# A transformer trunk on one core: other places for split weights, smaller first loads, and the last tokens in four pieces

## The chip, the cores and the metric

The kernel runs on one core of a Trainium2 chip. The metric is the device time of one execution in microseconds (us): the median of several runs, lower is better. Beside the timed runs one execution was taken by the hardware profiler; all rows below are from that one.

## What is computed

One sequence of 256 tokens with 1,024 features passes two layers: causal attention (16 heads) with a SwiGLU, then an mLSTM (8 heads) with a second SwiGLU. Every sub-layer has an RMS norm before it and a residual add behind it; a last RMS norm ends the trunk. All arrays are float32. Cut to what matters here:

```python
def swiglu(xn, w_gate_up, w_down):
    gu = jnp.einsum('bsd,df->bsf', xn, w_gate_up)
    g, u = gu[..., :D_FF], gu[..., D_FF:]          # D_FF = 2816
    return jnp.einsum('bsf,fd->bsd', jax.nn.silu(g) * u, w_down)

h = h + moba_mixer(rmsnorm(h, attn_norm[0]), attn_w_qkv[0], attn_w_o[0], cos, sin)
h = h + swiglu(rmsnorm(h, ffn_norm[0]), ffn_w_gate_up[0], ffn_w_down[0])
h = h + mlstm_mixer(rmsnorm(h, mlstm_norm[0]), mlstm_w_in[0], mlstm_b_gates[0], mlstm_head_norm[0], mlstm_w_out[0])
h = h + swiglu(rmsnorm(h, ffn_norm[1]), ffn_w_gate_up[1], ffn_w_down[1])
return rmsnorm(h, final_norm)
```

## The kernel before

**Weights.** All weights are cut into units of 128 x 1024 floats (512 KB), listed by `unit_names` in the order of their use. A unit is loaded by SyncE's queue (SP) into one of 4 `raw` buffers (`load`, L133 to L144). Then ScalarE (ACT) rounds it to `wh` (L159) and VectorE (DVE) makes the rest, `wl` = raw - `wh` (L150): a float32 value as a sum of two numbers of the type float32r, which TensorE (PE) multiplies fast. `wh` and `wl` rotate through 8 buffers each of 4,096 bytes per partition (L155). Activations are split in the same way: `xh` and `xl` (L206, L207) hold the normed input, `hh` and `hl` (L652, L653) a hidden block of a SwiGLU. A product is three matmuls (`mm3`, L188): high x high, high x low, low x high.

**Where the tiles lie.** Pools are laid one behind another, with small filling tiles (`pad`) between some of them. In the built program each `raw`, `wh` and `wl` buffer begins at a multiple of 256 bytes in its partition; `xh`, `xl`, `hh` and `hl` begin 192 bytes past such a multiple.

**The order of TensorE's work** is the order in which the code is written; for most of the program a scheduler orders the other engines' instructions. A matmul has a stationary operand (loaded before it, 128 x 128) and a moving one (128 x 256 or 128 x 512).

- At the start 16 small matmuls warm TensorE; `first_block` then multiplies x, piece by piece (k = 0 to 7, 128 features each), with attention's first query and key weights: per k four blocks of six matmuls of 256 columns, each needing its quarter of the weight unit. x is not normed here. The norm's square sums (`square`, L211) are taken on ScalarE and added up on GpSimd (POOL, L219, L221), and the factor is applied to the results.
- A SwiGLU (`ffn`) has 22 hidden blocks. A **pair block** (`pair_block`) makes one block's gate and up values: 48 matmuls of 256 columns with `xh`/`xl` moving and weights stationary. A **down step** multiplies one hidden block with its part of the down matrix. In the first SwiGLU it is 24 matmuls of 256 columns with `hh`/`hl` moving and weights stationary. In the second the result stands with tokens in partitions, so that the last norm can work along the free dimension: 12 matmuls of 512 columns with weights moving and `hh`/`hl` stationary (`tok_tiles`, L390). Pair blocks and down steps follow each other in turns; the down step of block j - 6 runs beside block j. The last down steps stand alone behind the last pair block.
- The end (`finish_last`, L395): for each half of the tokens (t = 0, 1) and each half of the columns (c = 0, 1; one PSUM bank each) the last two down steps are done, then ScalarE squares and sums the bank. The two sums are added on VectorE (L408), GpSimd takes the power -1/2 (L410), ScalarE and VectorE scale one half each (L414, L416), and SP stores both (L418).

```python
            for c in range(2):
                cs = slice(c * 512, (c + 1) * 512)
                for i, (u, h) in enumerate(steps):
                    tok_tiles(acc, u, h, t, c, i == len(steps) - 1)
                sq = fp.tile([P, 512], F32, name="fsq", tag="fsq")
                nc.scalar.activation(sq, acc[2 * t + c], AF.Square, scale=1.0 / 32.0, accum_out=ss[:, c:c + 1])
```

Of the kernel before, what the change touches and what calls it, by code (L numbers as in the profile page):

```python
# [9 lines left out]
F32 = mybir.dt.float32  # L10
F32R = mybir.dt.float32r
BF16 = mybir.dt.bfloat16
AF = mybir.ActivationFunctionType
ALU = mybir.AluOpType
PSUM = bass.MemoryType.PSUM

P = 128
S = 256
NF = 8
NJ = 22  # L20
EPS = 1e-6
# [7 lines left out]
LAG = 6  # L29
# [10 lines left out]

V_ATTN, V_FFN0, V_MLSTM, V_FFN1, V_HEAD, V_BIAS, V_END = 0, 8, 16, 24, 32, 40, 56

def unit_names():
# [31 lines left out]
def trunk_kernel(ctx: ExitStack, tc: tile.TileContext, x, w, wg, fw, tab, out):  # L77
    nc = tc.nc
    names = unit_names()
# [14 lines left out]
    w_pool = ctx.enter_context(tc.tile_pool(name="wsplit", bufs=WBUFS))  # L94
    xp = ctx.enter_context(tc.tile_pool(name="xp", bufs=1))
    sm = ctx.enter_context(tc.tile_pool(name="small", bufs=2))
# [23 lines left out]
    XV = xp.tile([P, V_END + NF * S], F32, name="XV")  # L120
# [6 lines left out]
    split = {}  # L127

    def pieces(c):
        return (slice(0, S), slice(S, 1024)) if c == 0 else (slice(0, 1024),)  # L130

    def load(upto):
        while len(raws) < min(upto, len(names)):  # L133
            c = len(raws)
            raw = raw_pool.tile([P, 1024], F32, name="raw", tag="raw")
            if c < NF:
                o = V_END + c * S
                o = slice(o if c else 0, o + S)
                nc.sync.dma_start(out=XV[:, o], in_=x[:, o])
            for sl in pieces(c):  # L140
                nc.sync.dma_start(out=raw[:, sl], in_=w[c][:, sl])
            if c == 5:
                nc.sync.dma_start(out=tab_t, in_=tab)
            raws.append(raw)  # L144
# [7 lines left out]
    def prefetch(upto, lag=0):  # L152
        for c in range(len(split), min(upto, len(names))):
            load(c + RAW - 1)
            wh, wl = (w_pool.tile([P, 1024], F32R, name=a, tag=a) for a in ("wh", "wl"))  # L155
            split[c] = (wh, wl)
            cuts = (0, S, 512, 1024) if c == 0 else (0, 512, 1024) if c == 1 else (0, 1024)
            for sl in map(slice, cuts, cuts[1:]):
                nc.scalar.copy(wh[:, sl], raws[c][:, sl])  # L159
                lows.append((c, sl))  # L160
                if len(lows) > lag:
                    low(*lows.pop(0))
                if c < NF and sl.start == 0:
                    n0.feed(c)
        while len(lows) > lag:
            low(*lows.pop(0))
# [15 lines left out]
    mhalf = const.tile([P, 2], F32, name="mhalf")  # L182
# [5 lines left out]
    def mm3(o, a, b, start, stop):  # L188

        mm(o, a[0], b[0], start, False)  # L190
        mm(o, a[0], b[1], False, False)
        mm(o, a[1], b[0], False, stop)

    class Norm:
# [15 lines left out]
        def square(self, f):  # L210

            xs = X[:, f:f + 2].rearrange("p f t -> p (f t)")
            if self.ssum is None:
                self.ssum = sm.tile([P, 512], F32, name="ssum", tag="ssum", bufs=1)
                nc.scalar.activation(self.ssum, xs, AF.Square)
            else:
                sq = sm.tile([P, 512], F32, name="sq", tag="sq")
                nc.scalar.activation(sq, xs, AF.Square)
                nc.gpsimd.tensor_add(self.ssum, self.ssum, sq)  # L219
            if f == NF - 2:  # L220
                nc.gpsimd.tensor_add(self.ssum[:, 0:S], self.ssum[:, 0:S], self.ssum[:, S:512])  # L221

        def mean(self):
            ms = acc_tile()
# [162 lines left out]
        n.feed(7)  # L387
        return n

    def tok_tiles(acc, u, h, t, c, last):  # L390

        sl, cs = slice(t * P, (t + 1) * P), slice(c * 512, (c + 1) * 512)
        mm3(acc[2 * t + c], (h[0][:, sl], h[1][:, sl]), (u[0][:, cs], u[1][:, cs]), False, last)

    def finish_last(acc, steps, fwb, fp):  # L395

        for t in range(2):
            ss = sm.tile([P, 4], F32, name="ss", tag="fss")
            y = fp.tile([P, 1024], F32, name="yout", tag="yout")
            for c in range(2):  # L400
                cs = slice(c * 512, (c + 1) * 512)
                for i, (u, h) in enumerate(steps):
                    tok_tiles(acc, u, h, t, c, i == len(steps) - 1)
                sq = fp.tile([P, 512], F32, name="fsq", tag="fsq")
                nc.scalar.activation(sq, acc[2 * t + c], AF.Square, scale=1.0 / 32.0, accum_out=ss[:, c:c + 1])
                if c == 0:
                    nc.vector.tensor_mul(y[:, cs], acc[2 * t], fwb[:, cs])
            nc.vector.scalar_tensor_tensor(out=ss[:, 2:3], in0=ss[:, 0:1], scalar=EPS, in1=ss[:, 1:2],  # L408
                                           op0=ALU.add, op1=ALU.add)
            nc.gpsimd.tensor_tensor(out=ss[:, 3:4], in0=ss[:, 2:3], in1=mhalf[:, 0:1], op=ALU.pow)  # L410
            for c in range(2):
                cs = slice(c * 512, (c + 1) * 512)
                if c == 0:
                    nc.scalar.activation(y[:, cs], y[:, cs], AF.Copy, scale=ss[:, 3:4])  # L414
                else:
                    nc.vector.scalar_tensor_tensor(out=y[:, cs], in0=acc[2 * t + 1], scalar=ss[:, 3:4],  # L416
                                                   in1=fwb[:, cs], op0=ALU.mult, op1=ALU.mult)
                nc.sync.dma_start(out=out[t * P:(t + 1) * P, cs], in_=y[:, cs])  # L418


    n = n0 = Norm(V_ATTN)
# [45 lines left out]
    with ExitStack() as actx:  # L467
# [147 lines left out]
        acc = []  # L615
        blocks = [tok_block("av", 2 * i, n, v_evict, lambda *a: main.later(A_D6, *a)) for i in range(2)]
        parts = {0: [blocks[0]], 1: [islice(blocks[1], V1), blocks[1]]}
# [14 lines left out]
        n = finish(acc, [(unit("ao", 3, 1), ot.pop(7))], V_FFN0)  # L632


    def ffn(l, n, fp, col):
        hid = {}
        last_phase = col is None
        if last_phase:
            fwb = fp.tile([P, 1024], F32, name="fwb", bufs=1)
# [19 lines left out]
        acc = []  # L659

        def down(j):
            u = unit(f"d{l}", j // 2, j % 2)
            if not acc:
                acc.extend(acc_tile() for _ in range(4))
                if last_phase:

                    for b in range(4):
                        t, c = b // 2, b % 2
                        for i in range(4):
                            nc.tensor.matmul(acc[b][:, i * P:(i + 1) * P], lhsT=X[:, 4 * c + i, t * P:(t + 1) * P],  # L670
                                             rhs=ident, start=i == 0, stop=False, is_transpose=True,
                                             skip_group_check=True)
            if last_phase:
                for b in range(4):
                    tok_tiles(acc, u, hid[j], b // 2, b % 2, False)
                hid.pop(j)
            else:
                out_tiles(acc, u, hid.pop(j), j == 0, False)

        nd = 0  # L680
        for j in range(4, NJ):
# [3 lines left out]
            b = ps_tile() if j > 4 else acc_tile()  # L685
# [3 lines left out]
        last = (NJ - 2, NJ - 1) if last_phase else (NJ - 1,)  # L689
# [12 lines left out]
    with ExitStack() as mctx:  # L702
# [188 lines left out]
        acc = []  # L891
# [127 lines left out]
```

## Time and profile before

| | |
|---|---|
| median of 3 runs | 607.2 us (607.06 to 607.92) |
| the profiled execution | 605.8 us, of which 604.0 us lie between its first and last instruction (the span) |
| TensorE matmul | 590.7 us busy (98% of the span), 4,524 matmuls |
| VectorE, ScalarE, GpSimd | 415.8, 340.9 and 77.9 us busy |
| granted TensorE clock | 0.996 in the mean |
| DMA engines | 58.7% of their time in transfers |

"Busy" counts an instruction from its start to its end. Matmuls overlap: one that is shown with 0.28 us is followed by the next after 0.11 or 0.12 us, so a busy share near 100% doesn't say that TensorE is at its peak. What a matmul costs in a row of matmuls is the interval from its start to the start of the next.

### The profile page before, as it was taken

Reading aid. Unit: us, or ns where it says so; the run is one execution under the profiler, and the core shown is the slowest. Engines: PE = TensorE matmul, PEld = TensorE weight load, DVE = VectorE, ACT = ScalarE, POOL = GpSimd, SP = SyncE. Lnnn points to the kernel's source line nnn. Section 1 sums busy time; section 2 is a strip of 40 time slices with the busy share of each in tenths; the row PEclk is TensorE's granted clock in tenths of the full one; section 3 lists DMA queues with packets and bytes.
Section 4 is the critical chain, followed back from the end, with each engine's and each line's share of the span. In section 5 each row is a group of like instructions: output and inputs, shape, how many; then the busy total and the mean of one; then the engine's idle time right before and its main releaser. Section 6 shows DMA issues by size and latency. Waiting matters only on the chain.

```text
span 604.0 us, 11573 instructions
## 1 busy us (share of the span) xinstructions
PE 590.7 (98%) x4524; PEld 561.2 (93%) x4524; DVE 415.8 (69%) x663; ACT 340.9 (56%) x611; POOL 77.9 (13%) x81
## 2 busy tenths in 40 slices
PE   8997999999999999999999999999999999999995
PEld 7987998999999999999999878999999999999984
DVE  5899898797866666566388678858776656556532
ACT  7645999767544444445275478846754444444412
POOL 2574320042000000000031300114100000000000
PEclk9999999999999999999999999999999999999999
DMA  8778965358655656555428868343955555565401
GB/s 312 286 216 260 263 200 159 140 180 305 214 196 189 207 179 206 183 201 190 163 81 302 255 218 222 110 141 117 308 175 200 178 187 197 175 194 190 141 0 69
DMA packets 36342, 116.39 MB, mean 193 GB/s; under 512 B 4544, under 2 KB 7360, under 8 KB 36288
## 3 DMA queue, kind: packets, MB, share of 16 engines
q1 hardware_dynamic: 36288, 115.66, 58.7%
q8 instruction: 35, 0.57, 0.4%
q14 instruction: 19, 0.16, 0.1%
HBM read 105.15 MB, written 1.05 MB: 176 GB/s over the span
## 4 chain that ended last, share of the span: by engine, by line
PE 83%; DVE 5%; ACT 4%; DMA 3%; issue 2%; SPq 1%; POOL 1%; POOLq 0%; ACTq 0%; DVEq 0%
PE ps L186 46%; PE acc L186 36%; DMA raw<-w 2%; DVE wl L150 2%; DMA stk<-u 1%; ACT wh L159 1%; ACT p L535 1%; ACT p L545 1%; DVE xl L207 1%; DVE u L449 1%; DVE VT L507 0%; PE ps L555 0%; SPq L452 0%; POOL sh L487 0%; POOL qk L488 0%
## 5 line engine op out<-in xcount | busy, mean ns | idle before, releaser
L150 DVE TENSOR_TENSOR wl<-raw,wh 128x1024 fp32r<-128x1024 f32 (+2 forms) x199 | 244.1, 1233 | 109.5 <-ACT wh L159 106.9
L159 ACT CAST wh<-raw 128x1024 fp32r<-128x1024 f32 (+2 forms) x199 | 205.5, 1038 | 184.9 <-PE ps L186 102.7
L186 PE MATMUL ps<-xh,wh 128*128 128x256 f32 x864 | 242.4, 281 | 0.8 <-ACT wh L159 0.8
L186 PE MATMUL ps<-xh,wl 128*128 128x256 f32 x864 | 241.0, 279 | 0.5 <-DVE wl L150 0.5
L186 PE MATMUL ps<-xl,wh 128*128 128x256 f32 x864 | 240.7, 279 | 0.0
L186 PEld LDWEIGHTS ps<-xh,wh 128*128 128x128 f32 x864 | 163.0, 189 | 2.1 <-ACT wh L159 1.2
L186 PEld LDWEIGHTS ps<-xh,wl 128*128 128x128 f32 x864 | 163.7, 189 | 1.1 <-DVE wl L150 1.1
L186 PEld LDWEIGHTS ps<-xl,wh 128*128 128x128 f32 x864 | 163.0, 189 | 0.7
L186 PE MATMUL acc<-hh,wh 128*128 128x256 f32 x176 | 48.6, 276 | 0.0
L186 PE MATMUL acc<-hl,wh 128*128 128x256 f32 x176 | 48.6, 276 | 0.0
L186 PE MATMUL acc<-hh,wl 128*128 128x256 f32 x176 | 48.6, 276 | 0.0
L219 POOL TENSOR_TENSOR ssum<-ssum,sq 128x512 f32<-128x512 f32 x12 | 20.5, 1708 | 198.6 <-issue 163.7
L644 DVE TENSOR_TENSOR tgu<-ps,R 128x512 f32<-128x512 f32 x42 | 28.6, 690 | 20.9 <-PE ps L186 20.9
L186 PE MATMUL acc<-wh,xh 128*128 128x512 f32 x96 | 39.0, 406 | 0.0
L186 PE MATMUL acc<-wh,xl 128*128 128x512 f32 x96 | 37.8, 393 | 0.0
L186 PE MATMUL acc<-wl,xh 128*128 128x512 f32 x96 | 37.7, 392 | 0.0
L186 PE MATMUL acc<-wh,hh 128*128 128x512 f32 x88 | 34.7, 394 | 0.0
L186 PE MATMUL acc<-wl,hh 128*128 128x512 f32 x88 | 34.7, 394 | 0.0
L186 PE MATMUL acc<-wh,hl 128*128 128x512 f32 x88 | 34.3, 390 | 0.0
L186 PEld LDWEIGHTS acc<-hl,wh 128*128 128x128 f32 x176 | 33.0, 188 | 0.0
L186 PEld LDWEIGHTS acc<-hh,wl 128*128 128x128 f32 x176 | 33.0, 188 | 0.0
L186 PEld LDWEIGHTS acc<-hh,wh 128*128 128x128 f32 x176 | 33.0, 188 | 0.0
(180 smaller groups left out, 853.8 us busy)
## 6 DMA issues: line engine op xcount, KB each, us to landing
raw<-w SPq DMA_DIRECT2D x195, 512.0 KB, 4.2
stk<-u SPq DMA_DIRECT2D x24, 192.0 KB, 4.3
stk<-u SPq DMA_DIRECT2D x24, 128.0 KB, 4.2
stk<-u SPq DMA_DIRECT2D x24, 64.0 KB, 3.6
out<-yout SPq DMA_DIRECT2D x4, 256.0 KB, 2.2
XV<-x SPq DMA_DIRECT2D x7, 128.0 KB, 6.2
tab_t<-tab SPq DMA_DIRECT2D x1, 708.0 KB, 6.9
fwb<-fw SPq DMA_DIRECT2D x1, 512.0 KB, 3.5
```

The source lines that it names most:

```text
L150: nc.vector.tensor_sub(wl[:, sl], raws[c][:, sl], wh[:, sl].bitcast(F32))
L159: nc.scalar.copy(wh[:, sl], raws[c][:, sl])
L186: nc.tensor.matmul(o, lhsT=lhsT, rhs=rhs, start=start, stop=stop, skip_group_check=True)
L207: nc.vector.scalar_tensor_tensor(out=self.l[:, f], in0=X[:, f], scalar=wc, in1=self.h[:, f].bitcast(F32), op0=ALU.mult, op1=ALU.subtract)
L219: nc.gpsimd.tensor_add(self.ssum, self.ssum, sq)
L449: nc.vector.tensor_sub(u[:, 512:1024], mv, u[:, 0:512].bitcast(F32))
L535: nc.scalar.activation(pt[:, sl], pt[:, sl], AF.Exp, bias=mx[:, t:t + 1], scale=-1.0, accum_out=ss[:, t:t + 1])
L545: nc.scalar.activation(pt[:, sl], pt[:, sl], AF.Copy, scale=ss[:, t:t + 1])
L644: nc.vector.tensor_mul(t.rearrange("p (g t) -> p g t", g=2), bank.rearrange("p (g t) -> p g t", g=2), n.R2())
```

## The change

Four parts. (1) The split buffers become 4,352 bytes long; in the units listed in `MOVING` (down units 0 to 15 of the second SwiGLU) the data begin 128 bytes into the buffer. (2) Weight units 0 and 1 are loaded in three pieces (256, 256 and 512 columns) and split in three; x's first two pieces are issued from ScalarE's queue. (3) The first norm's square sums are added on VectorE. (4) In `finish_last` the second half of the tokens is done in four pieces of 256 columns, in turns in the two banks. Each piece's sum is added to the running one, each piece is multiplied by the norm's weights before the factor is known, and the factor is applied at the end: for t = 0 by VectorE with one store, for t = 1 by VectorE (672 columns, stored by SP) and ScalarE (352 columns, stored from its own queue).

```diff
+MOVING = tuple(("d1", j // 2, j % 2) for j in range(NJ - LAG))
...
     def pieces(c):
-        return (slice(0, S), slice(S, 1024)) if c == 0 else (slice(0, 1024),)
+        return (slice(0, S), slice(S, 512), slice(512, 1024)) if c < 2 else (slice(0, 1024),)
...
-                nc.sync.dma_start(out=XV[:, o], in_=x[:, o])
+                (nc.scalar if c < 2 else nc.sync).dma_start(out=XV[:, o], in_=x[:, o])
...
-            wh, wl = (w_pool.tile([P, 1024], F32R, name=a, tag=a) for a in ("wh", "wl"))
+            o = 32 if names[c] in MOVING else 0
+            wh, wl = (w_pool.tile([P, 1088], F32R, name=a, tag=a)[:, o:o + 1024] for a in ("wh", "wl"))
             split[c] = (wh, wl)
-            cuts = (0, S, 512, 1024) if c == 0 else (0, 512, 1024) if c == 1 else (0, 1024)
+            cuts = (0, S, 512, 1024) if c < 2 else (0, 1024)
...
+            eng = nc.vector if self.col == V_ATTN else nc.gpsimd
...
-                nc.gpsimd.tensor_add(self.ssum, self.ssum, sq)
+                eng.tensor_add(self.ssum, self.ssum, sq)
             if f == NF - 2:
-                nc.gpsimd.tensor_add(self.ssum[:, 0:S], self.ssum[:, 0:S], self.ssum[:, S:512])
+                eng.tensor_add(self.ssum[:, 0:S], self.ssum[:, 0:S], self.ssum[:, S:512])
...
+    def tok_tiles(acc, u, h, t, cs, last):
+
+        sl, c = slice(t * P, (t + 1) * P), cs.start // 512
+        o = acc[2 * t + c][:, cs.start - c * 512:cs.stop - c * 512]
+        mm3(o, (h[0][:, sl], h[1][:, sl]), (u[0][:, cs], u[1][:, cs]), False, last)
...
+            parts = ((0, 512), (512, 1024)) if t == 0 else ((0, S), (512, 768), (S, 512), (768, 1024))
+            for i, cs in enumerate(slice(*p) for p in parts):
+                for j, (u, h) in enumerate(steps):
+                    tok_tiles(acc, u, h, t, cs, j == len(steps) - 1)
+                a = acc[2 * t + cs.start // 512][:, cs.start % 512:(cs.stop - 1) % 512 + 1]
                 sq = fp.tile([P, 512], F32, name="fsq", tag="fsq")
-                nc.scalar.activation(sq, acc[2 * t + c], AF.Square, scale=1.0 / 32.0, accum_out=ss[:, c:c + 1])
-                if c == 0:
-                    nc.vector.tensor_mul(y[:, cs], acc[2 * t], fwb[:, cs])
...
+                nc.scalar.activation(sq[:, 0:cs.stop - cs.start], a, AF.Square, scale=1.0 / 32.0,
+                                     accum_out=ss[:, i:i + 1])
+
+                if i > 0:
+                    nc.vector.scalar_tensor_tensor(out=ss[:, 3 + i:4 + i], in0=ss[:, i:i + 1],
+                                                   scalar=EPS if i == 1 else 0.0,
+                                                   in1=ss[:, 0:1] if i == 1 else ss[:, 2 + i:3 + i],
+                                                   op0=ALU.add, op1=ALU.add)
+                nc.vector.tensor_mul(y[:, cs], a, fwb[:, cs])
+            n = 2 + len(parts)
+            nc.gpsimd.tensor_tensor(out=ss[:, 7:8], in0=ss[:, n:n + 1], in1=mhalf[:, 0:1], op=ALU.pow)
+            rows = out[t * P:(t + 1) * P]
+            cut = 672 if t else 1024
+            nc.vector.tensor_scalar(y[:, 0:cut], y[:, 0:cut], ss[:, 7:8], None, op0=ALU.mult)
+            nc.sync.dma_start(out=rows[:, 0:cut], in_=y[:, 0:cut])
+            if t:
+                nc.scalar.activation(y[:, cut:], y[:, cut:], AF.Copy, scale=ss[:, 7:8])
+                nc.scalar.dma_start(out=rows[:, cut:], in_=y[:, cut:])
```

By the built program's addresses, the data of units 0 to 15 now begin at 128 past a multiple of 256 bytes; every other tile that a matmul reads keeps its place modulo 256. The 16 split buffers begin at multiples of 256 that are in turns even and odd.

How the change moves instructions on three engines follows from the built programs; line numbers are each program's own.

ScalarE at the program's start, before:

```order
L116 ACT_TABLE_LOAD
L116 ACTIVATE dummy<-warm 128x1
L206 ACTIVATE xh<-XV 128x256
L159 CAST wh<-raw 128x256 x2
L159 CAST wh<-raw 128x512
L206 ACTIVATE xh<-XV 128x256
L215 ACTIVATE ssum<-XV 128x512
L159 CAST wh<-raw 128x512 x2
```

And in the change (`XV` holds x, `xh` its scaled and rounded pieces):

```order
L143 DMA XV<-x 128x312
L120 ACT_TABLE_LOAD
L120 ACTIVATE dummy<-warm 128x1
L143 DMA XV<-x 128x256
L211 ACTIVATE xh<-XV 128x256
L164 CAST wh<-raw 128x256
L211 ACTIVATE xh<-XV 128x256
L221 ACTIVATE ssum<-XV 128x512
L164 CAST wh<-raw 128x256
L164 CAST wh<-raw 128x512
L164 CAST wh<-raw 128x256 x2
L164 CAST wh<-raw 128x512
```

Two DMA issues stand on ScalarE, and x's second piece with its square now stands ahead of the second quarter of the first weight unit.

VectorE at the program's end, before (`ss` holds the sums, `yout` the result, `fwb` the norm's weights):

```order
L407 TENSOR_TENSOR yout<-acc,fwb 128x512
L408 SCALAR_TENSOR_TENSOR ss<-ss 128x1
L416 SCALAR_TENSOR_TENSOR yout<-acc,ss,fwb 128x512
L407 TENSOR_TENSOR yout<-acc,fwb 128x512
L408 SCALAR_TENSOR_TENSOR ss<-ss 128x1
L416 SCALAR_TENSOR_TENSOR yout<-acc,ss,fwb 128x512
```

And in the change:

```order
L422 TENSOR_TENSOR yout<-acc,fwb 128x512
L418 SCALAR_TENSOR_TENSOR ss<-ss 128x1
L422 TENSOR_TENSOR yout<-acc,fwb 128x512
L422 TENSOR_TENSOR yout<-acc,fwb 128x256
L427 TENSOR_SCALAR yout<-yout,ss 128x1024
L418 SCALAR_TENSOR_TENSOR ss<-ss 128x1
L422 TENSOR_TENSOR yout<-acc,fwb 128x256
L418 SCALAR_TENSOR_TENSOR ss<-ss 128x1
L422 TENSOR_TENSOR yout<-acc,fwb 128x256
L418 SCALAR_TENSOR_TENSOR ss<-ss 128x1
L422 TENSOR_TENSOR yout<-acc,fwb 128x256
L427 TENSOR_SCALAR yout<-yout,ss 128x672
```

The first half's second product (512 columns) and its scaling (1024 columns) now stand among the products of the second half's pieces.

TensorE in the second half of the last tokens, in the change, around the start of the third piece, with what it waits for:

```order
L191 MATMUL acc<-wl,hh 128x256
L191 MATMUL acc<-wh,hl 128x256
L191 MATMUL acc<-wh,hh 128x256 [waits DVE_49]
L191 MATMUL acc<-wl,hh 128x256
L191 MATMUL acc<-wh,hl 128x256
```

Each piece is six such rows. The third piece's first matmul waits for VectorE's product of the first piece, which lies in the same bank, and the fourth's for that of the second. Before, the last twelve matmuls (128x512) waited for nothing.

## Rows read from the trace of the kernel before

**Rows 1.** Windows of the two SwiGLUs: stretch, length, busy us of each engine, PEclk, DMA, GB/s.

```profile
160.00:240.00 80.00, 80.00 (x709) 80.00 (x708) 49.56 (x61) 37.09 (x49) 0.00 (x0) 1.00 0.58 196
460.00:580.00 120.00, 120.00 (x861) 112.82 (x860) 71.05 (x86) 52.77 (x70) 0.00 (x0) 1.00 0.51 172
```

**Rows 2.** Chain of waits in the first SwiGLU: start us, us, what.

```profile
217.59 5.44 PE ps L186 x48
223.03 2.72 PE acc L186 x24
```

**Rows 3.** Chain of waits in the second SwiGLU, its first pair block and step.

```profile
449.36 5.66 PE ps L186 x48
455.01 2.77 PE acc L186 x12
```

**Rows 4.** Chain of waits in the second SwiGLU, its last pair block.

```profile
575.66 5.66 PE ps L186 x48
```

**Rows 5.** Timeline of TensorE in the mLSTM's output: start us, us, what.

```profile
405.07 0.28 PE L186 MATMUL acc<-yl,wh 128*128 128x256 f32 x1
...
405.41 0.28 PE L186 MATMUL acc<-yl,wh 128*128 128x256 f32 x1
...
405.64 0.38 PE L873 MATMUL ps<-tab_t,y 128*128 128x128 f32 x2
...
405.97 0.28 PE L186 MATMUL acc<-yl,wh 128*128 128x256 f32 x1
...
406.33 0.28 PE L186 MATMUL acc<-yl,wh 128*128 128x256 f32 x1
```

**Rows 6.** Timeline of TensorE in attention, behind a block of 512-column matmuls.

```profile
42.10 0.28 PE L186 MATMUL ps<-xh,wh 128*128 128x256 f32 x1
...
42.78 0.28 PE L186 MATMUL ps<-xh,wh 128*128 128x256 f32 x1
```

**Rows 7.** Timeline of the start, by engine (SP, ScalarE, TensorE).

```profile
2.10 0.43 SPq L139 DMA_DIRECT2D XV<-x  x1
...
0.71 1.28 ACT L116 ACT_TABLE_LOAD   x1 [0.71 <-PEq L1011]
...
3.05 0.51 ACT L206 ACTIVATE xh<-XV 128x256 fp32r<-128x256 f32 x1 [0.84 <-DMA XV<-x]
...
5.23 0.93 ACT L159 CAST wh<-raw 128x256 fp32r<-128x256 f32 x2 [1.24 <-DMA raw<-w]
6.06 0.51 ACT L206 ACTIVATE xh<-XV 128x256 fp32r<-128x256 f32 x1
...
9.69 0.39 PE L186 MATMUL ps<-xh,wl 128*128 128x256 f32 x1 [0.23 <-DVE wl L150]
```

**Rows 8.** Timeline of VectorE and TensorE in the first block's later part.

```profile
14.71 2.05 DVE L207 SCALAR_TENSOR_TENSOR xl<-XV,xh 128x256 fp32r<-128x256 f32 x2
...
21.56 0.39 PE L186 MATMUL ps<-xh,wl 128*128 128x256 f32 x1 [0.29 <-DVE wl L150]
```

**Rows 9.** Timeline of the end, all engines.

```profile
594.90 0.39 PE L186 MATMUL acc<-wh,hh 128*128 128x512 f32 x1
...
595.82 0.16 DVE L408 SCALAR_TENSOR_TENSOR ss<-ss 128x1 f32<-128x1 f32 x1 [0.68 <-ACT fsq L405]
...
597.31 0.68 DVE L407 TENSOR_TENSOR yout<-acc,fwb 128x512 f32<-128x512 f32 x1
...
597.42 0.39 PE L186 MATMUL acc<-wh,hl 128*128 128x512 f32 x1
597.90 0.60 ACT L405 ACTIVATE fsq<-acc 128x512 f32<-128x512 f32 x1
...
599.46 0.75 DVE L416 SCALAR_TENSOR_TENSOR yout<-acc,ss,fwb 128x512 f32<-128x512 f32 x1 [0.67 <-POOL ss L410]
```

**Rows 10.** Groups by line and shape, VectorE: count, busy us, mean ns of one, idle before.

```profile
L649 DVE TENSOR_TENSOR hd<-sil,tgu 128x256 f32<-128x256 f32 x44 | 18.1, 419 | 1.1 <-ACT sil L647 1.1
...
L889 DVE TENSOR_SCALAR og<-og 128x512 f32<-128x512 f32 x4 | 1.6, 421 | 0.8 <-ACT og L888 0.8
```

More of the change, by code (lines that the diff above doesn't have):

```diff
@@ L388, in finish @@
         return n
-    def tok_tiles(acc, u, h, t, c, last):
-        sl, cs = slice(t * P, (t + 1) * P), slice(c * 512, (c + 1) * 512)
-        mm3(acc[2 * t + c], (h[0][:, sl], h[1][:, sl]), (u[0][:, cs], u[1][:, cs]), False, last)
+    def tok_tiles(acc, u, h, t, cs, last):
+        sl, c = slice(t * P, (t + 1) * P), cs.start // 512
+        o = acc[2 * t + c][:, cs.start - c * 512:cs.stop - c * 512]
+        mm3(o, (h[0][:, sl], h[1][:, sl]), (u[0][:, cs], u[1][:, cs]), False, last)
     def finish_last(acc, steps, fwb, fp):
@@ L397, in finish_last @@
         for t in range(2):
-            ss = sm.tile([P, 4], F32, name="ss", tag="fss")
+            ss = sm.tile([P, 8], F32, name="ss", tag="fss")
             y = fp.tile([P, 1024], F32, name="yout", tag="yout")
[L400 to L403, printed above, removed]
-                sq = fp.tile([P, 512], F32, name="fsq", tag="fsq")
-                nc.scalar.activation(sq, acc[2 * t + c], AF.Square, scale=1.0 / 32.0, accum_out=ss[:, c:c + 1])
-                if c == 0:
-                    nc.vector.tensor_mul(y[:, cs], acc[2 * t], fwb[:, cs])
@@ L408, in finish_last @@
[L408 to L418, printed above, removed]
+            parts = ((0, 512), (512, 1024)) if t == 0 else ((0, S), (512, 768), (S, 512), (768, 1024))
@@ L674, in down @@
                 for b in range(4):
-                    tok_tiles(acc, u, hid[j], b // 2, b % 2, False)
+                    tok_tiles(acc, u, hid[j], b // 2, slice(b % 2 * 512, b % 2 * 512 + 512), False)
                 hid.pop(j)
```

## The prediction

> **What bounds the kernel now.** I read four views, in this order. First the windows: in two long stretches of the two SwiGLUs TensorE is busy for the whole time (80.00 of 80.00 us, 120.00 of 120.00) at a granted clock of 1.00, the 2.4 GHz level [rows 1]. Nobody is waited for there; what the stretch costs is the interval from one matmul's start to the next, and only a shorter interval makes it shorter. So, second, the chain of waits, which in such a stretch is a list of matmul runs. In the first SwiGLU a pair block (48 matmuls of 256 columns) takes 5.44 us, 113.3 ns each, and a down step (24 of 256 columns) 2.72 us, again 113.3 ns [rows 2]. In the second SwiGLU the same pair block takes 5.66 us, 117.9 ns each, and its down step (12 of 512 columns) 2.77 us, 231 ns each, or 115.4 ns per 256 columns [rows 3, 4]. The same instructions on the same tiles at the same clock are 4% slower. The only thing between them that the first SwiGLU doesn't have is the 512-column down step, with weights as the moving operand.
>
> Third, the timeline, for how a matmul changes from one interval to the other. Before two transposes at 405.64 us three intervals take 0.34 us, after them 0.36 us [rows 5], and the slower ones go on until TensorE next stops. The other way, after the 512-column matmuls of attention's value projection, six intervals from 42.10 to 42.78 us take 0.68 us, 113.3 ns each [rows 6]. So there are two steady rates for one instruction, the state is kept, and what runs between decides which one follows; after 512-column matmuls both occur. Fourth, the two ends, where engines do wait: TensorE for the first loads and splits [rows 7, 8], and the program's end for a chain of small operations behind the last matmul [rows 9].
>
> **The offset.** Today every split buffer starts at a multiple of 256 bytes, while `xh`, `xl`, `hh` and `hl` start 192 bytes past one. Where activations move (pair blocks, first SwiGLU's down steps), the moving operand stands 192 bytes past the stationary one, modulo 256; in the second SwiGLU's down steps it stands 64 past. The change puts the weights of down units 0 to 15 at 128, and 128 minus 192 is again 192. The 256 extra bytes leave every other tile where it was, modulo 256. I take it that the down step then behaves as the first SwiGLU's: 2.72 us, and that the pair block behind it stays at 5.44 us. There are 16 such periods (pair blocks from 449.36 to 575.66 us, one each 8.42 us [rows 3, 4]).
> - Pair blocks: 16 x (5.66 - 5.44) = 3.5 us saved. Bounds: 0, if the slow rate stays, and 3.5.
> - Down steps: 16 x (2.77 - 2.72) = 0.8 us saved. No row has this operand pair at 512 columns, so the bounds are wide: at a column per cycle of the 2.4 GHz level a step can't be under 12 x 0.213 = 2.56 us (3.4 us saved), and at twice the slow pair-block interval it is 2.83 us (1.0 us lost). I take 2.72, the nearest row with the same difference of addresses.
>
> The rows show that a matmul is slowed by something other than its own columns. Against this stands the Trainium skill, "TensorE: Matmul & The Clock Gate", section "Step-by-step: what each phase is for": TensorE has two independent SBUF read ports, and loading the next weights takes no read bandwidth from the running matmul. By that rule no start address can matter, both terms above are 0, and the sum is the first rival's 607.5 where the rows make it 603.2.
>
> **The start.** x's first two pieces go to ScalarE's queue, weights 0 and 1 come in three loads. On SP the second x piece was issued at 2.10 us [rows 7]; on ScalarE it stands behind the first issue (0.43 us like that one), the table load of 1.28 us that began at 0.71 [rows 7] and a small activation, so about 2.6 us. Behind it on ScalarE is queued the second quarter of weight 0, whose cast must now wait for x's second piece, its scaling and its square; today it runs at 5.23 us, before that scaling at 6.06 [rows 7]. If that piece lands as fast as x's first (issued as the program began, near 0.7 us, and used at 3.05 [rows 7]) the quarter is ready near 6.1 us, if it takes as long as today's may (issue 2.10, used 6.06) near 7.8. The remaining 18 matmuls of k = 0 take 2.1 us at 117.9 ns, so k = 1 begins between 8.2 and 9.9 us, against 9.69 us less two intervals, 9.45, now (the matmul at 9.69 is k = 1's third, and the last that waits there [rows 7]): -1.2 to +0.5 us.
> VectorE takes over the four adds of the square sums from GpSimd. Beside those adds its two `xl` operations took 2.05 us [rows 8], where an operation of 256 columns otherwise takes 0.42 [rows 10]; so it pays some 2.5 us (three of 512 columns at 0.68 [rows 9], one of 256) and gets much of that back. It now also makes `wl` 4 ahead of `xl` 5. TensorE's wait of 0.29 us for a `wl` at 21.56 us [rows 8] should go: -0.3 to 0. Together -1.5 to +0.5; I take -0.7, since part may be lost again in attention, whose waits come from another chain.
>
> **The end.** The last 128 tokens start at 594.90 us, twelve matmuls of 512 columns, the last at 597.42: 0.229 us each [rows 9]. Now they are 24 of 256 columns in four pieces of 0.69 us, in turns in two banks, and piece 3's first matmul waits for VectorE's product of piece 1, piece 4's for that of piece 2. VectorE's queue at that point: the small sum at 595.82 (0.16 us) as before, then the product of the first half's second 512 columns, moved here (0.68), to 596.66; product of piece 1 (0.42 by a 256-column row [rows 10]), to 597.08. Piece 3 could have begun at 594.90 + 12 x 0.115 = 596.27: TensorE waits 0.8 us, and ends it at 597.8. VectorE goes on with the 1024-column scaling (one of 512 took 0.42 [rows 10]; between 0.42 and 0.84, taken 0.69), the small sum 0.16, product of piece 2 0.42: 598.35. Piece 4 waits another 0.55 and ends at about 599.05, against 597.65 now. From there the rest was 597.65 to 600.21 us [rows 9], 2.56 us; it gets shorter by about 0.2 (a square of 256 columns, where 512 took 0.60) and 0.25 (0.75 us for 512 columns from PSUM becomes about 0.50 for 672 from SBUF). 599.05 + 2.1 = 601.15: 0.9, with wake-ups 1.0 us later. The last two transfers move the same bytes as before, so I give nothing for the second queue. Bounds: -0.45 if VectorE keeps up, +1.4 if the scaling takes 0.84 and the tail gives nothing back.
>
> **Sum:** -3.5 - 0.8 - 0.7 + 1.0 = -4.0 us, from the profiled execution's 605.8 to 601.8. That execution lies 1.4 us under the median of the runs, 607.2, so the median goes to 603.2.
>
> **The rivals.**
> - The offset does nothing, as by the rule of the two ports: -0.7 + 1.0, the time is 607.5. For it: both operand pairs differ by 64 modulo 128, so if only 128 bytes count nothing changes. Against: intervals differ by 4% with nothing waited for. Chance 0.13.
> - The down step gets shorter, but the pair blocks behind it stay slow. The state behind 512-column matmuls goes both ways [rows 3, 6], and at the period's two edges the address differences are still others. -0.8 - 0.7 + 1.0: 606.7, or 604.1 with the down step at its lower bound. Chance 0.18.
> - Slower: the slow rate moves into the first SwiGLU. The longer buffers put every second stationary tile 256 bytes off, modulo 512, and the matmuls that enter this stretch come at other moments. It decides at its first pair block, behind the transposes of its norm; if that block takes 5.66 us, all 18 blocks (0.22 each) and 22 down steps (24 x 4.6 ns = 0.11 each) cost 6.4 us: 609.6. Against: tiles of both kinds run at either rate today, and the rate has entered well there. Chance 0.09.
>
> **The numbers.** The forecast, 603.2, has 0.60; its own range is 600.5 (down step near its lower bound or a better start) to 604.8. A measurement tells about 0.2%, 1.2 us, from no change. Under 606.0 lie nearly all of the forecast and a quarter of the second rival: 0.64. Between 606.0 and 608.4 lie the rest of that rival and most of the first: 0.26. Above, the third and a little of the first: 0.10. The range 600.5 to 607.7 leaves out the third rival, the upper end of the first and the lowest of the forecast, 0.17.
>
> **What would show it.** In the chain of the second SwiGLU pair blocks of 5.44 us and down steps of 2.72 or less show the offset right; 5.66 with a shorter down step the second rival, 5.66 and 2.77 the first. In the first SwiGLU anything but 5.44 shows the third. In the timeline's end two waits of TensorE on VectorE between 596 and 598.5 us of today's scale show the new wait, none shows me wrong there. At the start, ScalarE's wait for x's second piece and no gap near 21 us. A shift in attention's waits that eats the start would make that term 0.

## The result and the profile after

The changed kernel takes 604.3 us in the median of 4 runs (602.42 to 604.71), the kernel before on the same chip 607.55 us (607.06 to 607.92): a ratio of 0.9927 with a 95% interval of 0.9899 to 0.9954, so about 4.4 us less by the ratio and 3.2 us by the medians. The forecast was 603.2, with 600.5 to 607.7 as its range. The profiled execution took 604.25 us with a span of 602.5, 1.5 us under the span before. Why the profiles differ by less than the medians is told among the reasons, under attention and the mLSTM.

The windows of the two SwiGLUs (stretch, length, busy us of each engine, PEclk, DMA, GB/s), after:

```profile
160.00:240.00 80.00, 80.00 (x708) 80.00 (x707) 50.02 (x62) 37.58 (x50) 0.00 (x0) 1.00 0.58 199
460.00:580.00 120.00, 120.00 (x878) 112.38 (x877) 72.17 (x87) 52.98 (x71) 0.00 (x0) 1.00 0.50 172
```

They read as before [rows 1]: TensorE busy all the time, clock 1.00. But the second stretch, of the same length, now holds 878 matmuls where it held 861. The chain of waits (start us, us, what) shows which became shorter:

```profile
217.07 5.44 PE ps L191 x48
222.51 2.72 PE acc L191 x24
...
449.97 5.45 PE ps L191 x48
455.43 2.79 PE acc L191 x12
...
573.57 5.45 PE ps L191 x48
579.02 13.75 PE acc L191 x60
```

The first SwiGLU is as it was [rows 2]. In the second every pair block behind a down step takes 5.45 us instead of 5.66, and the down steps take 2.79 instead of 2.77 [rows 3, 4]: a period of 8.24 us instead of 8.42. Here is the gain.

The pair block at 449.36 us [rows 3] is not the second SwiGLU's first. It is the first behind a down step; two pair blocks stand ahead of it. In the kernel before:

```profile
433.97 5.44 PE acc L186 x48
439.41 5.45 PE ps L186 x48
444.86 1.75 PE acc L670 x16
446.60 2.75 PE acc L186 x12
```

These two pair blocks (the first is shown under `acc`, its bank comes from there) run at the fast rate, here and in all 14 profiles. Then come 16 transposes, which put the residual into the accumulators, and the first down step, and from there the blocks are slow. So in these 16 periods the slow rate comes in with the first down step.

The start, by engine (start us, us, engine, line, operation):

```profile
0.72 0.41 ACTq L143 DMA_DIRECT2D XV<-x  x1
...
1.17 1.28 ACT L120 ACT_TABLE_LOAD   x1 [1.17 <-PEq L1024]
1.24 0.38 ACTq L143 DMA_DIRECT2D XV<-x  x1
...
3.79 0.51 ACT L211 ACTIVATE xh<-XV 128x256 fp32r<-128x256 f32 x1 [1.13 <-DMA XV<-x]
...
7.68 0.38 PE L191 MATMUL ps<-xh,wl 128*128 128x256 f32 x1 [0.23 <-DVE wl L154]
...
12.53 0.39 PE L191 MATMUL ps<-xh,wl 128*128 128x256 f32 x1 [0.48 <-DVE wl L154]
...
19.42 0.48 DVE L212 SCALAR_TENSOR_TENSOR xl<-XV,xh 128x256 fp32r<-128x256 f32 x1
```

The second piece of x is issued at 1.24 us, while the table load runs, not behind it. The first piece is used at 3.79 us, where it was 3.05 [rows 7]. TensorE's waits near 9 us [rows 7] and at 21.56 us [rows 8] are gone, and one at 12.53 us stands there instead. One `xl` of VectorE takes 0.48 us at 19.42; beside GpSimd's adds two of them took 2.05 [rows 8].

The end, all engines:

```profile
591.42 0.60 ACT L414 ACTIVATE fsq<-acc 128x512 f32<-128x512 f32 x1 [10.26 <-PE acc L191]
...
592.14 0.69 DVE L422 TENSOR_TENSOR yout<-acc,fwb 128x512 f32<-128x512 f32 x1 [10.52 <-ACT fsq L414]
...
592.60 0.28 PE L191 MATMUL acc<-wh,hh 128*128 128x256 f32 x1
...
593.53 0.39 ACT L414 ACTIVATE fsq<-acc 128x256 f32<-128x256 f32 x1
593.59 1.02 DVE L422 TENSOR_TENSOR yout<-acc,fwb 128x512 f32<-128x512 f32 x2
...
594.52 0.74 DVE L427 TENSOR_SCALAR yout<-yout,ss 128x1024 f32<-128x1024 f32 x1
594.66 0.39 PE L191 MATMUL acc<-wh,hh 128*128 128x256 f32 x1 [0.54 <-DVE yout L422]
...
595.72 0.19 PEld L191 LDWEIGHTS acc<-wh,hh 128*128 128x128 f32 x1 [0.29 <-DVE yout L422]
595.73 0.38 PE L191 MATMUL acc<-wh,hh 128*128 128x256 f32 x1
...
596.42 0.28 PE L191 MATMUL acc<-wh,hl 128*128 128x256 f32 x1
...
598.12 0.57 DVE L427 TENSOR_SCALAR yout<-yout,ss 128x672 f32<-128x672 f32 x1 [0.33 <-POOL ss L424]
```

Each bank is squared first and multiplied after that (591.42 and 592.14 us are the first half's first bank). The third and the fourth piece begin late, each behind a product on VectorE. From the first matmul of the last 128 tokens to the end of the span it is 602.5 - 592.60 = 9.90 us, where it was 604.0 - 594.90 = 9.10 [rows 9]. The spans are known to 0.1 us.

Following the same matmuls of the program through both profiles puts the 1.5 us of span in places: -0.95 at the start (by 25.8 us), +0.42 in attention, nothing in the first SwiGLU, +1.10 in the mLSTM, -2.87 in the second SwiGLU, +0.80 at the end.

### The profile page after: what moved, and what is told of

Read it like the earlier page. It is cut to its first block, busy times and chain, and to the rows that moved or that the text cites. A ratio compares the mean times of both kernels' runs of the same rounds, so it can differ in the third digit from the quotient of the medians.

```text
span 602.5 us, 11621 instructions
## 1 busy us (share of the span) xinstructions
PE 587.8 (98%) x4536; PEld 557.4 (93%) x4536; DVE 415.6 (69%) x674; ACT 340.3 (56%) x615; POOL 71.0 (12%) x77
## 4 chain that ended last, share of the span: by engine, by line
PE 75%; DMA 8%; DVE 7%; ACT 5%; issue 3%; SPq 2%; POOLq 0%; POOL 0%; ACTq 0%; DVEq 0%
PE ps L191 43%; PE acc L191 31%; DMA raw<-w 4%; DMA stk<-u 3%; DVE wl L154 3%; ACT wh L164 1%; DVE u L462 1%; SPq L465 1%; SPq L466 1%; ACT xh L211 1%; ACT p L548 1%; DMA XV<-x 1%; PE ps L568 0%; ACT u L458 0%; DVE qk L499 0%
## 5 line engine op out<-in xcount | busy, mean ns | idle before, releaser
L154 DVE TENSOR_TENSOR wl<-raw,wh 128x1024 fp32r<-128x1024 f32 (+1 forms) x200 | 243.5, 1223 | 109.6 <-ACT wh L164 109.2
L164 ACT CAST wh<-raw 128x1024 fp32r<-128x1024 f32 (+1 forms) x200 | 205.6, 1034 | 178.0 <-PE ps L191 96.1
L225 POOL TENSOR_TENSOR ssum<-ssum,sq 128x512 f32<-128x512 f32 x9 | 16.2, 1806 | 186.9 <-issue 163.7
L191 PE MATMUL acc<-wh,hh 128*128 128x512 f32 (+1 forms) x92 | 35.5, 386 | 0.6 <-DVE yout L422 0.5
L191 PE MATMUL acc<-wh,hl 128*128 128x512 f32 (+1 forms) x92 | 35.4, 384 | 0.0
L191 PE MATMUL acc<-wl,hh 128*128 128x512 f32 (+1 forms) x92 | 35.3, 384 | 0.0
```

Of the source, the lines that this page charges most:

```text
L154: nc.vector.tensor_sub(wl[:, sl], raws[c][:, sl], wh[:, sl].bitcast(F32))
L191: nc.tensor.matmul(o, lhsT=lhsT, rhs=rhs, start=start, stop=stop, skip_group_check=True)
L225: eng.tensor_add(self.ssum, self.ssum, sq)
```

## The experiments

There are twelve runs; two of them repeat a kernel. A time is compared with that of the kernel before, timed beside it on the same chip. Runs 5, 6, 9 and 10 have one time each (608.33, 606.35, 606.77 and 607.29 us), which settles nothing; they stand here for their traces. A table behind the runs has the stretches of all 14 profiles, which tell more than the times.

**1. No unit moved.**

```diff
-MOVING = tuple(("d1", j // 2, j % 2) for j in range(NJ - LAG))
+MOVING = ()
```

> The change with no unit moved (the buffers stay 4,352 bytes long, all data begin at the buffer's start). If the 128-byte offset of the down weights sets the matmuls' rate: pair blocks of the second SwiGLU go back to 5.66 us and down steps to 2.77, 16 x (0.21 - 0.02) = 3.0 us more than the change, about 607.3. If the longer buffers (every second one off by 256 modulo 512) do it: 5.45 and 604.3. If the rate is what the stretch happens to be entered with: either, and not the same in other variants.

0.9985 of the time before (0.9968 to 1.0002). The chain in the second SwiGLU:

```profile
489.41 2.77 PE acc L191 x12
492.17 5.66 PE ps L191 x48
```

The slow rate is back in all 16 periods, with start, end and buffer length as in the change. So the offset makes the gain, and the length alone does nothing. Whether the offset would do it in buffers of the old length, no run shows.

**2. The offset alone.** The kernel before with this:

```diff
+MOVING = tuple(("d1", j // 2, j % 2) for j in range(NJ - LAG))
...
-            wh, wl = (w_pool.tile([P, 1024], F32R, name=a, tag=a) for a in ("wh", "wl"))
+            o = 32 if names[c] in MOVING else 0
+            wh, wl = (w_pool.tile([P, 1088], F32R, name=a, tag=a)[:, o:o + 1024] for a in ("wh", "wl"))
```

> The kernel before with the longer buffers and the moved units only. If the offset sets the rate: 5.45 and 2.79 in all 16 periods, 3.0 us less than before, about 604.5. If start or end have a part in it: 5.66 and 2.77, 607.5.

0.9979 (0.9961 to 0.9997). In the chain:

```profile
491.87 2.79 PE acc L190 x12
494.66 5.46 PE ps L190 x48
```

The rate is as expected, and the stretch 145.81 us. The time is not: 1.3 us less by the ratio (0.2 to 2.4), where 3.0 were expected. In the profile attention and mLSTM took 72.63 and 102.26 us, 1.5 and 1.1 over their means, and in attention the granted clock was the lowest of all profiles (behind the table). Whether that belongs to this kernel or to the moment was not found out.

**3. The old end.** `finish_last` as before, the rest as in the change.

> The change with the old end. If the two waits of TensorE on VectorE cost what the traces show (9.90 us from the last 128 tokens' first matmul to the end, 9.10 before): 0.8 us faster than the change, 603.5. If the shorter tail behind the last matmul is worth as much as the waits: the same, 604.3.

0.9926 (0.9897 to 0.9955): no difference to the change's 0.9927 that these runs can tell. The profile can: 8.89 us from the last 128 tokens' first matmul to the end, not 9.90, and no wait of TensorE there.

**4. The old start.** Loads, cuts and square sums as before, the rest as in the change.

> The change with the old start (loads, cuts, square sums). If the start's gain of 0.95 us at 25.8 us reaches the end: 605.2. If attention and the mLSTM swallow it: 604.3, and the matmuls of both kernels stand at the same times behind the mLSTM.

0.9973 (0.9952 to 0.9993). Matmul 240 of the program (in attention's value projection) begins at 36.43 us, like the two other profiles with the old start (36.81, 36.38). With the new start it lies between 34.98 and 36.53 in 11 profiles, mean 35.64. So 0.9 us is won by there; what follows scatters by more (the table below), and whether the 0.9 us reaches the end no single profile can tell. The time without the new start, 0.9973 where the change has 0.9927 and 0.9942 (run 11), points to more than 0.9 us, but the intervals overlap.

What each part is worth in the whole time, these runs do not settle. By the ratios the offset alone gains 1.3 us, start and end without it (run 1) 0.9, the offset with the start (run 3) 4.5, each with 1.0 to 1.8 us to either side.

**5, 6. Other offsets.**

```diff
-            o = 32 if names[c] in MOVING else 0
+            o = 16 if names[c] in MOVING else 0
```

and 48 in the second.

> The change with the down weights 64 bytes into their buffers instead of 128. The moving operand then stands 128 past the stationary one, modulo 256; with the change it is 192, before it was 64. If the rate needs the difference 192 that the pair blocks have: pair blocks of 5.66 us, steps near 2.77, and 148.7 us from the first down step to the last 128 tokens. If any place but the buffer's start will do: 5.45 and 2.79, 145.8 us.

> The same with 192 bytes: both operands stand at the same place modulo 256. If the rate needs the difference 192: 5.66 us and 148.7. If any other place than the start will do: 5.45 and 145.8. If reads from the same place collide: steps above 2.80 us too.

The chain at 64 bytes:

```profile
490.15 2.77 PE acc L191 x12
492.92 5.65 PE ps L191 x48
```

and at 192:

```profile
488.32 2.75 PE acc L191 x12
491.06 5.66 PE ps L191 x48
```

Of the four offsets (0 is run 1) only 128 bytes leaves the fast rate behind the step, as the difference of 192 would have it. Its step is the longest of the four.

**7. Down steps of 256 columns.**

```diff
-                    tok_tiles(acc, u, hid[j], b // 2, slice(b % 2 * 512, b % 2 * 512 + 512), False)
+                    for q in range(2):
+                        o = b % 2 * 512 + q * S
+                        tok_tiles(acc, u, hid[j], b // 2, slice(o, o + S), False)
```

> The change with the second SwiGLU's 20 separate down steps made of 24 matmuls of 256 columns each in the place of 12 of 512. If a 256-column matmul with this operand pair runs at the fast rate: steps of 2.72 us, 20 x 0.07 = 1.4 us off the stretch, 144.4 us. If the moving weights go at the slow rate in that form: 2.83, and pair blocks of 5.66 behind them, 149.9 us.

0.9986 (0.9970 to 1.0002): the gain is lost.

```profile
489.89 2.74 PE acc L191 x24
492.63 5.65 PE ps L191 x48
```

Neither expectation held whole: the step itself runs fast, and the block behind it slowly. The operands, their places and the difference of 192 are those of the change; only the number of columns is another. So the difference of addresses, on which the prediction rested, does not decide by itself.

**8, 12. Another order of the last pieces.** The third quarter of the second half goes first, its last quarter at the very end:

```diff
...
+        part(1, slice(512, 768))
+        part(0, slice(0, 512))
+        part(0, slice(512, 1024))
+        tail(0)
+        part(1, slice(0, 512))
+        part(1, slice(768, 1024))
+        tail(1)
```

> The change with the pieces at the end in another order: third quarter of the second half of the tokens first, then the whole first half, then the second half's first 512 columns, its last quarter at the very end. No piece then follows a piece of its own bank. If the waits for the bank are what the end lost: no idle time of TensorE in the last matmuls, last matmul to the end about 6.0 us as in the change, and the end is some 1.0 us shorter than in the change (0.2 us than with the old end). If VectorE's queue is the limit: the waits go, and the time from the last matmul to the end grows by as much.

> The change with the pieces at the end in the order without bank waits, again, beside the change on one chip. If the end's 0.9 us counts: 0.15% faster than the change, 0.9915 of the time before. If other waits move by more than that: no difference that this measurement tells.

The end in the first of the two runs:

```profile
594.05 0.39 PE L191 MATMUL acc<-wh,hl 128*128 128x512 f32 x1
594.12 0.55 POOL L426 TENSOR_TENSOR ss<-ss,mhalf 128x1 f32<-128x1 f32 x1 [166.09 <-DVE ss L418]
594.28 0.28 PE L191 MATMUL acc<-wh,hh 128*128 128x256 f32 x1
...
594.75 0.75 DVE L429 TENSOR_SCALAR yout<-yout,ss 128x1024 f32<-128x1024 f32 x1
594.85 0.28 PE L191 MATMUL acc<-wh,hl 128*128 128x256 f32 x1
...
596.09 0.15 DVE L418 SCALAR_TENSOR_TENSOR ss<-ss 128x1 f32<-128x1 f32 x1
...
596.91 0.57 DVE L429 TENSOR_SCALAR yout<-yout,ss 128x672 f32<-128x672 f32 x1 [0.33 <-POOL ss L426]
```

No matmul waits. From the transposes ahead of the first down step to the end it is 154.78 us (154.79 in the second run), with the change 155.71 and 155.70: 0.9 us shorter, where 1.0 was expected. Against the old end in the same kernel (run 3, 154.70) 0.2 us was expected, and nothing is gained: the last small sum now stands behind VectorE's scaling and a product, from 594.75 to 596.09, and from the last matmul to the end it is 601.2 - 594.85 = 6.35 us, with the change 602.5 - 596.42 = 6.08. In the times, 0.9919 (0.9897 to 0.9941) and, beside the change on one chip, 0.9933 (0.9911 to 0.9956) against the change's 0.9942 (0.9923 to 0.9961): no difference that can be told.

**9. The other operand moved.** The weights at their old place, the hidden blocks 128 bytes further:

```diff
-MOVING = tuple(("d1", j // 2, j % 2) for j in range(NJ - LAG))
+MOVING = ()
...
+            pad(fp, 32)
             fwb = fp.tile([P, 1024], F32, name="fwb", bufs=1)
```

> The change with all weights back at their buffers' start, and the hidden blocks of the second SwiGLU 128 bytes further on instead. The down steps' moving operand then stands 192 past the stationary one, modulo 256, as with the change, but both lie elsewhere. If the difference between the two decides: pair blocks of 5.45 us, steps of 2.79, 145.8 us. If the place of the weights themselves decides: 5.66, 2.77 and 148.7 us.

```profile
475.48 5.66 PE ps L191 x48
481.14 2.80 PE acc L191 x12
483.93 5.46 PE ps L191 x48
489.39 2.79 PE acc L191 x12
492.18 5.66 PE ps L191 x48
```

Neither: the pair blocks are fast and slow in turns, through all periods (147.86 us).

**10. Steps of 256 columns, weights at their old place.**

> Down steps of 24 matmuls of 256 columns as in the run before of that kind, but with all weights at their buffers' start, so that the difference is 64. If the rate of the pair block hangs on the moment at which the step hands over: steps and blocks may change apart, steps of 2.72 to 2.83 us, blocks of 5.45 or 5.66. If 256-column steps with moving weights always leave the slow rate behind them: 5.65 again and 148.6 us.

```profile
490.05 2.72 PE acc L191 x24
492.77 5.66 PE ps L191 x48
```

Here too it goes in turns, steps of 2.72 and 2.83 us, blocks of 5.66 and 5.46. A step keeps the rate of the block ahead of it, and the block behind the step takes the other one. The same code, period after period, with two results: what is kept from one handover to the next decides along with the addresses.

**11. The change again.**

> The change itself beside the next kernel and the kernel before on one chip. 0.993 of the time before, as in the first measurement; 145.8 us from the first down step to the last 128 tokens, and 34.3 us to the 240th matmul. What the stretches with waits for loads (attention, mLSTM) take should differ by up to 2 us from the first profile.

0.9942 (0.9923 to 0.9961), the stretch again 145.81 us. Attention and mLSTM lie within 0.1 us of the first profile. Matmul 240 begins at 35.76 us, where 34.3 was expected; the first profile has 35.86, so the expected figure fits neither.

The handovers, as the intervals between the starts of successive matmuls in ns (D the end of a down step, P the start of the pair block behind it; one period each, the others of its kind differ by up to 3 ns in a matmul):

```
before, always                   D 230 231 227   P 117 118 118 118 117   slow
change, always                   D 231 236 228   P 122 116 114 113 113   fast
run 7, always                    D 113 113 118   P 114 118 118 117 118   slow
run 9, block ahead fast          D 231 236 229   P 117 119 117 118 118   slow
run 9, block ahead slow          D 236 230 236   P 117 117 120 115 115   fast
run 10, block and step fast      D 114 113 113   P 119 119 117 119 117   slow
run 10, block and step slow      D 118 117 117   P 122 115 115 113 113   fast
```

The fast rate is entered through one matmul of 119 to 122 ns, then 115 or 116. The slow one is there at once, or within two matmuls.

The stretches in us (start: to matmul 240, the 243rd that TensorE's records show; attention: matmuls 240 to 720, the 723rd; mLSTM: from its first block to the second SwiGLU's; SwiGLU 2: from the last transposes ahead of its first down step to the last 128 tokens' first matmul; end: from there, with spans to 0.1 us; runs 8 and 12, whose order of the last matmuls differs, have the last two as a sum):

| profile | start | attention | mLSTM | SwiGLU 2 | end |
|---|---|---|---|---|---|
| before | 36.81 | 70.62 | 99.78 | 148.68 | 9.10 |
| change, and again (11) | 35.86, 35.76 | 71.05, 70.96 | 100.88, 100.98 | 145.81 in both | 9.90, 9.89 |
| 1: no offset | 34.98 | 72.47 | 99.98 | 148.68 | 9.88 |
| 2: offset alone | 36.38 | 72.63 | 102.26 | 145.81 | 9.12 |
| 3: old end | 35.36 | 70.31 | 99.82 | 145.81 | 8.89 |
| 4: old start | 36.43 | 71.23 | 100.85 | 145.81 | 9.98 |
| 5: 64 bytes | 35.81 | 71.28 | 101.03 | 148.80 | 9.87 |
| 6: 192 bytes | 35.63 | 70.69 | 100.60 | 148.64 | 9.84 |
| 7: steps of 256 | 36.53 | 71.15 | 100.88 | 148.58 | 9.88 |
| 8, 12: other order | 35.17, 35.76 | 70.33, 71.35 | 101.91, 102.80 | 154.78, 154.79 | |
| 9: hidden blocks moved | 35.75 | 70.16 | 102.44 | 147.86 | 9.79 |
| 10: 256, old place | 35.44 | 71.95 | 101.66 | 147.57 | 9.87 |

Where TensorE waits for nobody, a stretch of the same kernel repeats to 0.01 us. Where it waits for loads and other engines, attention spreads over 2.5 us and the mLSTM over 3.0.

In attention the clock goes with it. The stretch from 36 to 107 us before, then with the change (columns as in [rows 1]; the granted clock stands third from the end):

```profile
36.00:107.00 71.00, 66.48 (x482) 61.68 (x481) 63.78 (x158) 57.83 (x150) 21.96 (x14) 0.98 0.77 214
36.00:107.00 71.00, 65.35 (x482) 60.21 (x481) 63.31 (x159) 57.25 (x150) 22.09 (x13) 1.00 0.80 213
```

The clock is 1.00 in the first profile of the change alone. It is 0.98 in seven profiles (attention 70.16 to 71.28 us), 0.95 in five, run 11 among them (70.96 to 72.47), and 0.93 in run 2 (72.63). It falls from the 2.4 to the 1.2 GHz level near 60 us, behind a stretch in which TensorE is mostly idle: before, it was busy for 1.56 of the 4 us from 56 to 60, and the clock of the next 4 us was 0.66. With the change it was busy for 1.70 us there and the clock stayed at 1.00, so what decides is not shown. Over the mLSTM the clock is 1.00 in all profiles.

## Why the prediction was right, and where it was not

**The pair blocks: right in size.** 16 x (5.66 - 5.44) = 3.5 us were forecast, 16 x (5.66 - 5.45) = 3.4 us came, and run 1 gives them back, run 2 has them alone. The rule of the Trainium skill ("TensorE: Matmul & The Clock Gate", section "Step-by-step: what each phase is for"), that loading weights takes nothing from the running matmul, would leave start addresses no part in the rate, as the prediction drew from it. Run 1 against the change, 5.66 against 5.45 us with only start addresses changed, shows that they have one; whether a weight load is what takes the time, no run shows.

**The reason given for it: wrong.** The step that failed is the one that "the down step then behaves as the first SwiGLU's", from the difference of 192 between the operands' places. With the same difference run 7 leaves the slow rate and run 9 both in turns. What the runs show in its place: two steady rates, kept until something disturbs them, and a handover whose outcome hangs on addresses, on columns and on the rate that was there before. That the change gets the fast one each time is shown; by which quantity, stays open, and the moment of the handover is not excluded. Since the reason doesn't hold, it was luck that 128 bytes, the only one of the four offsets that works, was the one tried. In the first block at the start the same kernel ran either way: the 24 matmuls of one k (k = 3, 4, 5) took 2.72 us each in the first profile of the change and 2.83 in run 11.

**The down steps: wrong by sign, small.** Forecast 0.8 us saved ("I take 2.72, the nearest row"), measured 16 x (2.79 - 2.77) = 0.3 us lost. It lies within the bounds that were given, 2.56 to 2.83. The 512-column matmuls mostly alternate between 231 and 236 ns where before they took 225 to 237, irregularly. The second rival, a shorter step with slow blocks behind it, is what run 6 does (2.75 and 5.66), not the change; the first rival (5.66 and 2.77) is run 1.

**The start: right in size, by the other of its two terms.** Forecast -0.7, measured -0.95 in the profile, -0.9 by the means of 11 profiles against 3. Of this the loads were given -1.2 to +0.5 us and the adds on VectorE -0.3 to 0.

The loads gave nothing that these profiles show. The second x piece was put at 2.6 us, behind the table load; it was issued at 1.24 and scaled at 4.51, without the wait of ScalarE that was expected. In turn x's first piece is used 0.74 us later. The first matmul of k = 1 begins at 8.94 us, before at 8.96 (the prediction's 9.45, two intervals back from 9.69, has its waits in it). Between these two profiles k = 1 then took 2.72 us where 3.42, and k = 2 lost 0.66 to the wait at 12.53. But over all profiles k = 3 begins at 14.26 to 15.50 us with the new start and at 14.52 to 15.21 with the old one, and both means are 14.8.

The gain lies behind it. From the start of k = 3 to that of k = 6 it is 9.41 to 9.72 us in the three profiles with the old start, 8.53 or some 8.85 in the eleven with the new one (by whether its matmuls went at the fast or the slow rate): 0.9 us in the mean, three times the bound that was given. There GpSimd's adds were, VectorE's `xl` took twice as long beside them, and TensorE waited for `wl` at 21.56 us; with the change it doesn't. So the rows put the gain on the adds. Run 4 takes back loads and adds together, so no run has the adds alone.

**The end: right.** Forecast +1.0, measured +0.80. Piece 3 was to begin 0.8 us late and piece 4 another 0.55: 594.66 against 592.60 + 12 x 0.115 = 593.98 is 0.68 us, and 595.73 against 594.66 + 0.69 is 0.38. The scaling took 0.74 us (0.69 taken). Run 3 undoes the loss, and run 8 does by giving no piece the bank of the piece two before it. Here stands the rule of the Trainium skill ("PSUM — Partial Sum Buffer", section "PSUM bank collisions raise a hardware error") that two engines are to be kept apart by bank and not by address. The program keeps to it, and the trace shows the price: a product waits for ScalarE's square of the same bank, though both only read it (the square runs from 591.42 us, the product begins at 592.14), and TensorE for the product of a piece in its bank, though it writes other columns. What happens without these waits, no run shows.

**Attention and the mLSTM: not in the forecast.** It gave nothing there; the profile lost 0.42 and 1.10 us. By the table both lie within the scatter: the profile of before had the shortest mLSTM of all 14, 99.78 us against a mean of 101.1, which fits with its execution lying 1.4 us under the median of the runs shown. The sum was made against that execution and then moved to the median, -4.0; by the medians it was -3.2, by the ratio -4.4. The parts that can be told, -2.87 in the second SwiGLU (forecast -4.3), -0.9 at the start and +0.80 at the end, make -3.0. By them the forecast was 1.0 us too much, and that the times came out nearer to it is luck.

**The third rival: not in this form.** From a pair block near the first SwiGLU's beginning to the first block of the mLSTM it is 156.40 us in all 14 profiles. But the slow rate did come into the block ahead of them, in runs 1, 4 and 5 (the row is run 4's):

```profile
124.56 14.16 PE ps L191 x120
```

With the change, 13.66 us for the same 120 matmuls:

```profile
123.82 13.66 PE ps L191 x120
```

The same 120 matmuls of the second SwiGLU take 14.13 us in all 14 profiles: there the slow rate stays, with the change too.

## What to carry to other kernels

Where TensorE is busy all the time at full clock, read the interval from one matmul's start to the next per block, and compare equal blocks in different places: 113 ns here and 118 there, with nobody waited for, is a gain that no busy share shows. Try operand start addresses one by one and look at the block behind the changed one too, since the changed one may itself get slower. Before cutting the last tiles into smaller pieces, count which pieces share a bank and what stands in the queue of the engine that must empty it; and judge a change of half a per cent by the stretches that repeat, not by one time. Look at the granted clock of a stretch before comparing it.

## What the runs showed of the hardware that was not expected

- One matmul, 256 columns with its own weight load, has two steady intervals at the same granted clock of 1.00, 113.3 and 117.9 ns, and a pair block of 48 keeps the one that it has after its first few matmuls.
- With a step between two blocks, the rate can flip at each handover: runs 9 and 10 go in turns through the whole stretch.
- A shift of one operand by 128 bytes is worth 0.21 us in a block of 48 matmuls that does not use that operand.
- An `xl` of 256 columns on VectorE took 0.48 us by itself; beside GpSimd's adds two took 2.05 us.
- In one kernel the granted clock falls near 60 us in one execution (0.95 from 36 to 107 us, run 11) and not in another (1.00, the first profile of the change).
- A DMA issued from ScalarE's queue is recorded at 1.24 us, inside the table load that runs there from 1.17 to 2.45.
